# A two-layer encoder on one core: differential values as one 512-wide product, pinned products in the FFN units, decays by minimum, and x added by an accumulating transfer

## The chip, the core and the metric

The kernel runs on one core of one Trainium2 chip. The metric is device microseconds of one execution. The three runs of the kernel before gave 1241.12, 1241.12 and 1242.99 us, a median of 1241.12; the execution that was profiled took 1242.97 us, of which 1241.2 us are the span from its first to its last instruction. The engines are named as the profile names them: PE multiplies matrices (PEld is its weight load), DVE works on vectors, ACT evaluates functions and copies, POOL and SP issue transfers here (POOL also fills memory with constants).

## What is computed

The reference is an encoder trunk of two layers on 512 tokens of width 1024, in float32:

```python
h = rms_norm(x, attn_norm_g[l])
rq, rk, rv, rg, dq, dk, dv = split(h @ w_in[l])             # seven projections, each 512 wide
ret = retention_bidir(rq, rk / 8, rv, lg_f, lg_b)            # 8 heads of 64, two decays per head
ret = rms_norm(ret, ret_norm_g[l]) * silu(rg)
da  = diff_attention(norm(dq), norm(dk), dv, lam, slopes)    # 4 heads: (A1 - lam * A2) v
da  = rms_norm(da, diff_norm_g[l]) * (1 - lam_init)
x = x + concat(ret, da) @ w_out[l]
h = rms_norm(x, ffn_norm_g[l])
x = x + (silu(h @ w_gate[l]) * (h @ w_up[l])) @ w_down[l]    # 2816 hidden columns
```

In retention the score of query t and key s is multiplied by `exp(lg_f * (t - s))` where s is not after t, and by `exp(lg_b * (s - t))` where it is; both exponents are negative or zero.

## The kernel before

The stream x lies transposed, as eight tiles of 128 features by 512 tokens. Every float32 operand of a product is split into a rounded high part and a low part (a copy on ACT, a subtraction on DVE), and a product is three matmuls, high by high, high by low and low by high (`mm3`, lines 207 to 209). A chunk of weights, 128 by 1024, is loaded by SP, cast by ACT (L194) and subtracted by DVE (L200).

A layer runs like this.

- **First projections.** Key and query tiles 0 and 1 of the differential attention (`project_first`), four PSUM banks over four chunks, while the squares of x are summed for the norm. The norm's scale `rstd` comes after them.
- **Early part.** `qk_tile` evicts such a bank (L372: u is the bank times `rstd`), sums the squares of each head's 64 rows on PE (L139, L140, into an aux bank), and scales and splits the tile. Behind the four tiles stand the first half of the differential values (`project_dv(0)`: weights 256 columns wide are the moving operand, the tokens of h are the stationary one) and two of the four gate projections.
- **Heads.** Each of four differential heads goes through four blocks of 128 queries. A block has two score products (L406, two matmuls each) into the two `sc` banks; DVE evicts each with its bias and a running minimum (L410), ACT exponentiates; after the softmax the block is transposed on PE (L422), split, and multiplied with the values. Between blocks stand "fillers", one step of a projection each: query and key tiles 2 and 3, the second half of the values, gates 2 and 3, and the first retention projections. `project_k` and `project_q` end a step with the projection; the eviction (the first line of `qk_tile`) belongs to the next step.
- **Retention.** Four pairs of heads (`ret_pair`), each in four steps. A pair's decays are `exp` of an argument made from two constant arrays (`ndist`, `dpos`; lines 478 to 484, on DVE). Fillers are the last retention projections and the attention half of the output projection (`project_out(0)`), eight tiles whose product is added on DVE to a tile of x that SP has loaded (L643). Then comes the other half (`project_out(1)`), with the sums of the last pair's norm (L139, L140) among its products.
- **FFN.** Four hidden tiles are done plainly; eighteen others in units of seven products of 256 columns (`seven`, matmuls on L803): six hidden tiles, then a second group's first tile, four down units, five tiles, a last group's first tile, four down units, and the rest. A unit uses one `acc` bank (pa) and one `sc` bank (px). In the left half of pa three products add up: g1·b11, copied by ACT (L808), then s2·t2, copied again (L811), then s3·t3, which DVE subtracts (L815). In the right half of px stands s1·t1, copied by ACT (L813). A hidden tile's result is later split for the down units (`first_parts`, `second_parts`, the casts on L753).

What sets the order: the program is written as generators, and a scheduler with a simulated timeline places every instruction on its engine's queue. Each engine then takes its queue in order. The scheduler respects data and a few added dependencies, so a text that is changed in one place moves instructions in others. Units are numbered by `turns[0]` from 1 in each layer.

Of the kernel before, what the change touches and what calls it, by code (L numbers as in the profile page):

```python
# [13 lines left out]
P = 128  # L14
D = 1024
T = 512
DEPTH = 2
# [31 lines left out]
CST_DIST, CST_DPOS, CST_QPOS = 0, 896, 1280  # L49
# [5 lines left out]
def encoder_kernel(ctx: ExitStack, tc: tile.TileContext, xT, wfirst, wsingle, wvv, wout, wgu, wdn, wds, prm, lam, cst, outT):  # L55
# [75 lines left out]
    dpos = cst_sb[:, CST_DPOS : CST_DPOS + 384]  # L131
# [145 lines left out]
    def prepare_small():  # L277
# [4 lines left out]
        used = prm_sb[:, PRM_DEC : PRM_DEC + 32]  # L282
        lam_sb = big("lam")
# [30 lines left out]
        consts.update(gk=gk, lg=lg, lamn=lamn, gq=gq, gd=gd, wk=wk, rs=rs)  # L314

    def layer(l, n1, h, x_src, first_raw):
# [27 lines left out]
        lg, lamn, gq, gd, wk, rs = (consts[k] for k in ("lg", "lamn", "gq", "gd", "wk", "rs"))  # L344
# [24 lines left out]
        def qk_tile(ps, col, early, stack):  # L369

            u = big("u")
            nc.vector.tensor_tensor(u, ps, rstd, op=ALU.mult)  # L372
# [10 lines left out]
        def project_v(which, half, get=acc_bank):  # L383

            w = [[t.rearrange("p (k f) -> p k f", f=256) for t in chunk(wvv[l, which, half, i])] for i in range(2)]
            for i in range(4):
                ps = get()[:, :256]
# [53 lines left out]
        def ret_pair(pr):  # L441
            qT, kT, v = rqs[pr], rks[pr], rv
            lgc = lambda d, hh: lg[:, l * 16 + d * 8 + 2 * pr + hh : l * 16 + d * 8 + 2 * pr + hh + 1]
            lgp = lambda d: lg[:, 32 + l * 8 + d * 4 + pr : 32 + l * 8 + d * 4 + pr + 1]
# [90 lines left out]
        def project_dv(half, get=acc_bank):  # L535
            for i, ps in project_v(1, half, get):
                hi = tpool.tile([P, 256], F32R, tag="dv", name=nm("dvh"), bufs=16)
                lo = tpool.tile([P, 256], F32R, tag="dv", name=nm("dvl"), bufs=16)
# [3 lines left out]
                if i % 2:  # L542
                    yield
# [51 lines left out]
        for _ in project_dv(0, out_bank):  # L595
            pass
# [31 lines left out]
        for _ in fillers(gate[:2]):  # L628
            pass
# [433 lines left out]
```

## Time and profile before

| what | value |
|---|---|
| median of three runs | 1241.12 us |
| profiled execution | 1242.97 us |
| its span | 1241.2 us |
| PE busy | 1231.5 us, 7954 matmuls |
| DVE busy | 990.4 us |
| ACT busy | 739.7 us |
| POOL busy | 80.6 us |
| TensorE clock granted | 1.000 |
| read from memory, written | 152.29 MB, 4.19 MB |

Of layer 0, the first projections end near 30 us, the heads run from 64 to about 190 us, retention to about 260 us, the plain hidden tiles to about 340 us and the units to about 560 us. Layer 1 repeats this some 615 us later.

How to read it: a row of the timeline has the start in microseconds, the duration, engine, line, operation, tiles (output, then inputs), shapes and count, and in brackets the idle time before it and what ended it. A matmul's recorded duration is longer than the distance to the next start, as matmuls are pipelined; so the distance between starts is the time that one costs. A row of grouped instructions ends in busy time and mean nanoseconds of one, and behind the second bar the idle time ahead of them.

### The profile page before, as it was taken

How to read it: one execution, taken by the hardware profiler on the slowest of the kernel's cores; microseconds unless marked ns; L12 is line 12 of the kernel's file. 1: busy time of each engine (PE TensorE's matmuls, PEld its weight loads, DVE VectorE, ACT ScalarE, POOL GpSimd, SP SyncE). 2: the span in 40 equal slices, each digit the busy share in tenths (PEclk: the TensorE clock that was granted, in tenths of full speed). 3: DMA queues.
4: the chain of work that ended last, by engine and by line, in shares of the span. 5: the costliest groups of instructions: out<-in, count | busy, mean ns of one | idle time of the engine just before them, and what ended most of it. 6: DMA issues, size and time to landing. Idle time of an engine off the chain costs nothing. (4 is left out here: it accounts for less than half of the span.)

```text
span 1241.2 us, 20513 instructions
## 1 busy us (share of the span) xinstructions
PE 1231.5 (99%) x7954; PEld 1111.5 (90%) x7954; DVE 990.4 (80%) x1638; ACT 739.7 (60%) x1282; POOL 80.6 (6%) x94
## 2 busy tenths in 40 slices
PE   9999999999999999999999999999999999999998
PEld 7878988788899999999888889987788999999997
DVE  6899768868978888887648997699689788798763
ACT  6778747555456556555538786465554565566551
POOL 1000000010011111110000000000100111111100
PEclk9999999999999999999999999999999999999999
DMA  7222122363266796793532122141632767867822
GB/s 262 85 68 69 50 83 81 118 162 102 64 164 161 156 222 158 164 220 99 166 111 85 52 85 64 56 136 63 175 102 69 176 148 179 205 161 182 207 78 94
DMA packets 67554, 157.82 MB, mean 127 GB/s; under 512 B 6144, under 2 KB 16640, under 8 KB 67456
## 3 DMA queue, kind: packets, MB, share of 16 engines
q1 hardware_dynamic: 52880, 130.90, 34.1%
q0 software_dynamic: 14144, 25.17, 12.4%
q8 instruction: 62, 1.02, 0.3%
q10 hardware_dynamic: 432, 0.44, 0.1%
q14 instruction: 36, 0.29, 0.1%
HBM read 152.29 MB, written 4.19 MB: 126 GB/s over the span
## 5 line engine op out<-in xcount | busy, mean ns | idle before, releaser
L194 ACT CAST hi<-raw 128x1024 fp32r<-128x1024 f32 (+2 forms) x115 | 113.5, 992 | 112.2 <-PE sc L208 42.4
L200 DVE TENSOR_TENSOR lo<-raw,hi 128x1024 fp32r<-128x1024 f32 (+2 forms) x116 | 132.6, 1147 | 30.9 <-ACT hi L194 30.5
L209 PE MATMUL acc<-h,lo 128*128 128x512 f32 (+1 forms) x344 | 135.0, 393 | 0.0
L208 PE MATMUL acc<-h,hi 128*128 128x512 f32 (+1 forms) x344 | 135.0, 392 | 0.0
L207 PE MATMUL acc<-h,hi 128*128 128x512 f32 (+1 forms) x344 | 134.7, 394 | 0.0
L803 PE MATMUL acc<-hi,hi 128*128 128x256 f32 x432 | 122.5, 284 | 0.9 <-ACT g L811 0.9
L803 PE MATMUL acc<-hi,lo 128*128 128x256 f32 x432 | 122.2, 283 | 0.0
L803 PE MATMUL acc<-lo,hi 128*128 128x256 f32 x432 | 122.2, 283 | 0.0
L760 DVE TENSOR_TENSOR lo<-s,hi 128x1024 fp32r<-128x1024 f32 (+1 forms) x78 | 88.9, 1140 | 39.0 <-ACT hi L759 38.9
L760 DVE TENSOR_TENSOR lo<-raw,hi 128x1024 fp32r<-128x1024 f32 (+1 forms) x78 | 89.0, 1141 | 30.7 <-ACT hi L759 26.4
L759 ACT CAST hi<-s 128x1024 fp32r<-128x1024 f32 (+1 forms) x78 | 76.6, 983 | 48.8 <-PE acc L803 37.7
L759 ACT CAST hi<-raw 128x1024 fp32r<-128x1024 f32 (+1 forms) x78 | 76.6, 982 | 41.4 <-PE acc L803 20.7
L803 PEld LDWEIGHTS acc<-hi,hi 128*128 128x128 f32 x432 | 82.9, 192 | 1.4 <-ACT g L811 1.3
L803 PEld LDWEIGHTS acc<-lo,hi 128*128 128x128 f32 x432 | 82.9, 192 | 0.1
L803 PEld LDWEIGHTS acc<-hi,lo 128*128 128x128 f32 x432 | 82.9, 192 | 0.0
L209 PEld LDWEIGHTS acc<-h,lo 128*128 128x128 f32 x344 | 65.0, 189 | 13.3
L207 PEld LDWEIGHTS acc<-h,hi 128*128 128x128 f32 x344 | 64.8, 189 | 13.4 <-DVE u L372 0.6
L208 PEld LDWEIGHTS acc<-h,hi 128*128 128x128 f32 x344 | 65.0, 189 | 12.9
L781 POOL DMA_DIRECT2D s<-in_wgu x36 | 43.5, 1207 | 433.3 <-DMA s<-in_wgu 243.6
L803 PE MATMUL sc<-b,s 128*128 128x256 f32 x480 | 69.0, 283 | 0.0
L803 PEld LDWEIGHTS sc<-b,s 128*128 128x128 f32 x480 | 62.6, 192 | 0.0
L106 ACT ACTIVATE sc<-sc,mx 128x512 f32<-128x512 f32 x64 | 46.0, 720 | 18.1 <-DVE mx L410 17.8
(260 smaller groups left out, 3713.1 us busy)
## 6 DMA issues: line engine op xcount, KB each, us to landing
s<-in_wgu SPq DMA_DIRECT2D x54, 512.0 KB, 5.5
s<-in_wgu POOLq DMA_DIRECT2D x36, 512.0 KB, 7.8
raw<-in_wgu SPq DMA_DIRECT2D x34, 512.0 KB, 4.8
raw<-in_wsingle SPq DMA_DIRECT2D x32, 512.0 KB, 3.6
raw<-in_wgu SPq DMA_DIRECT2D x36, 256.0 KB, 3.8
s<-in_wds SPq DMA_DIRECT2D x24, 384.0 KB, 3.4
raw<-in_wvv SPq DMA_DIRECT2D x16, 512.0 KB, 3.7
raw<-in_wout SPq DMA_DIRECT2D x16, 512.0 KB, 3.6
```

What stands on the lines that cost most here:

```text
L106: i = nc.scalar.activation(out, src, f, **kw).ins
L194: c = nc.scalar.copy(hi[:, s], raw[:, s])
L200: nc.vector.tensor_tensor(lo[:, s], raw[:, s], f32(hi[:, s]), op=ALU.subtract)
L207: first = nc.tensor.matmul(out, L[0], R[0], start=start, stop=False)
L208: nc.tensor.matmul(out, L[0], R[1], start=False, stop=False)
L209: nc.tensor.matmul(out, L[1], R[0], start=False, stop=stop)
L759: last_cast[0] = nc.scalar.copy(hi, raw).ins.name
L760: last_split[0] = nc.vector.tensor_tensor(lo, raw, f32(hi), op=ALU.subtract).ins.name
L781: nc.gpsimd.dma_start(sums, blocks[:, 0::3], accum_op=ALU.add)
L803: nc.tensor.matmul(ps[:, t], L[x1], R[x2], start=start and k + i == 0, stop=k == n // P - 1 and i == 2, skip_group_check=True)
```

## The change

- **Differential values 512 wide.** `project_dv` makes all 512 columns at once: four banks (two `o`, two `acc`), one per block of 128 tokens, over four chunks; it is run right after the first projections, one chunk ahead of the four `qk_tile` and one behind each. All four gates become fillers.
- **Evictions.** The four first tiles are evicted together, ahead of their `qk_tile`. `qk_tile` gets the evicted tile. For key tile 2 the eviction stands behind its own projection, ahead of the yield.
- **Pinned products, deferred splits.** In units 3 and 8, s1·t1 may start only after s2·t2. The `first_parts` of units 1, 2 and 12 are issued after the next unit's first four products.
- **Decays by minimum.** With d = t − s signed, the exponent is min(lg_f·d, −lg_b·d): a scaled copy on ACT and one operation on DVE per head.
- **x accumulated.** In the first half of the output projection ACT copies the bank into a tile, and POOL issues a transfer that adds the tile of x from memory to it.

```diff
+        nlgb = used[:, :16]
+        for l in range(DEPTH):
+            nc.vector.tensor_scalar(nlgb[:, l * 8 : l * 8 + 8], lg[:, l * 16 + 8 : l * 16 + 16], -1.0, None, op0=ALU.mult)
...
-        def qk_tile(ps, col, early, stack):
-
-            u = big("u")
-            nc.vector.tensor_tensor(u, ps, rstd, op=ALU.mult)
+        def qk_tile(u, col, early, stack):
             ss = aux_bank()
...
-            behind = big("behind")
-            nc.vector.tensor_tensor(behind[:, :384], ndist[:, C : C + 384], dpos, op=ALU.add)
             for hh in range(2):
                 arg = big("arg")
-                nc.vector.tensor_scalar(arg[:, :384], behind[:, :384], lgc(1, hh), -1.0, op0=ALU.mult, op1=ALU.mult)
-                nc.vector.scalar_tensor_tensor(arg[:, :384], dpos, lgc(0, hh), arg[:, :384], op0=ALU.mult, op1=ALU.add)
+                nc.scalar.activation(arg[:, :384], signed, AF.Copy, scale=lgm(hh))
+                nc.vector.scalar_tensor_tensor(arg[:, :384], signed, lgc(0, hh), arg[:, :384], op0=ALU.mult, op1=ALU.min)
                 func(arg[:, :384], arg[:, :384], AF.Exp)
...
-        def project_dv(half, get=acc_bank):
-            for i, ps in project_v(1, half, get):
...
+        def project_dv():
+            banks = [b() for b in (out_bank, out_bank, acc_bank, acc_bank)]
+            for c in range(4):
+                w = [t.rearrange("p (k f) -> p k f", f=512) for t in chunk(wdv[l, c])]
+                for i in ((2, 3, 0, 1) if c == 3 else range(4)):
+                    ps = banks[i]
+                    for k in range(2):
+                        kt = 2 * c + k
+                        mm3(ps, cut(h[kt], slice(None), slice(i * P, (i + 1) * P)), cut(w, slice(None), k), kt == 0, kt == KT - 1)
+                yield
+            dv[:] = [[None] * 4 for _ in range(2)]
+            for i in (2, 3, 0, 1):
+                ps = banks[i]
+                for half in range(2):
...
         def project_k(m):
             ps = project("dk", m)
-            yield
-            k[m] = qk_tile(ps, kgc, False, stack_two)
+            if m not in (2,):
+                yield
+            u = big("u")
+            nc.vector.tensor_tensor(u, ps, rstd, op=ALU.mult)
+            if m in (2,):
+                yield
+            k[m] = qk_tile(u, kgc, False, stack_two)
...
-        for (name, m), ps in zip(FIRST, first):
+        us = []
+        for ps in first:
+            us.append(big("u"))
+            nc.vector.tensor_tensor(us[-1], ps, rstd, op=ALU.mult)
+        early_dv = project_dv()
+        next(early_dv)
+        for i, ((name, m), u) in enumerate(zip(FIRST, us)):
             if name == "dk":
-                k[m] = qk_tile(ps, kgc, True, stack_two)
+                k[m] = qk_tile(u, kgc, True, stack_two)
             else:
-                q[m] = qk_tile(ps, gq[:, l, m : m + 1], True, stack_one)
-        for _ in project_dv(0, out_bank):
-            pass
+                q[m] = qk_tile(u, gq[:, l, m : m + 1], True, stack_one)
+            next(early_dv, None)
...
-        for _ in fillers(gate[:2]):
-            pass
...
-                [project_k(2), project_q(2), project_k(3), project_q(3), project_dv(1)]
-                + gate[2:]
+                [project_k(2), project_q(2), project_k(3), project_q(3)]
+                + gate
...
+                products(m, (3,) if m < early else (0, 1, 2, 3))
                 if half == 0:
-                    x.append(load_x(x_src, m))
-                products(m, (3,) if m < early else (0, 1, 2, 3))
-                residual(m, x[m], ps[m], *then)
+                    x.append(big("x", tag="qk", bufs=NQK))
+                    nc.scalar.copy(x[m], ps[m])
+                    nc.gpsimd.dma_start(x[m], x_src[m], accum_op=ALU.add)
+                else:
+                    residual(m, x[m], ps[m], *then)
...
-            product(pa, H1, s2, "t2", False)
+            done = product(pa, H1, s2, "t2", False)
             nc.scalar.copy(g[:, H2], pa[:, H1])
-            product(px, H2, s1, "t1", True)
+            product(px, H2, s1, "t1", True, done if number in (3,8) else None)
...
-                    if not (j == 0 and wait):
+                    if not (j == 0 and wait) and turns[0] - 1 not in (1,2,12):
                         later.pop()()
...
             next(unit)
+            if later and i in (1,2,12):
+                later.pop()()
             if i + 1 < len(units):
                 next(units[i + 1])
...
-        [ndist, np.maximum(d, 0), qpos, np.eye(P), kpos], 1
+        [ndist, d, qpos, np.eye(P), kpos], 1
```

With the new argument `behind`, `product` adds a dependency on the named matmul to each of its own. The weights of the values are laid out as four chunks of two feature tiles by 512 columns.

**PE in unit 3 of layer 0.** The bank pa is acc_3777 before and acc_3671 in the change, px is sc_3778 and sc_3672. Before, all of s1·t1 stood ahead of s2·t2, and s3·t3 follows s2·t2 at once:

```order
L803 MATMUL sc_3778<-hi_3426,lo_3766 128x256
L803 MATMUL acc_3777<-hi_3160,hi_3761 128x256
L803 MATMUL acc_3777<-lo_3161,hi_3761 128x256
L803 MATMUL acc_3777<-hi_3160,lo_3762 128x256
L803 MATMUL acc_3777<-hi_3261,hi_3761 128x256
L803 MATMUL acc_3777<-lo_3262,hi_3761 128x256
L803 MATMUL acc_3777<-hi_3261,lo_3762 128x256
```

In the change, g1·b11 on acc_3671 ends in the first two of these rows, two matmuls of the unit before (acc_3541) follow, and then s2·t2 begins:

```order
L829 MATMUL acc_3671<-bl_3310,hi_3655 128x256
L829 MATMUL acc_3671<-bh_3309,lo_3656 128x256
L829 MATMUL acc_3541<-lo_3325,hi_3533 128x256
L829 MATMUL acc_3541<-hi_3324,lo_3534 128x256
L829 MATMUL acc_3671<-hi_3054,hi_3655 128x256
L829 MATMUL acc_3671<-lo_3055,hi_3655 128x256
```

Behind its twelve matmuls now stand the twelve of s1·t1 on sc_3672, and only then s3·t3.

**ACT in unit 2 of layer 0.** Before, a chunk's cast and the cast of the earlier tile's first part stand ahead of the copy out of px (the copy is the row with sc):

```order
L811 COPY g_3649<-acc_3647 128x256
L759 CAST hi_3761<-raw_3752 128x1024
L753 CAST b_3705<-u_3703 128x256
L813 ACTIVATE u_3650<-sc_3648 128x256
L759 CAST hi_3765<-s_3751 128x1024
```

and in the change:

```order
L840 COPY g_3543<-acc_3541 128x256
L842 ACTIVATE u_3544<-sc_3542 128x256
L785 CAST hi_3655<-raw_3646 128x1024
L779 CAST b_3638<-u_3597 128x256
L785 CAST hi_3659<-s_3645 128x1024
```

The copy moved ahead of both casts. In unit 12 it likewise moved ahead of the first part's cast.

**PE in the first head of layer 0.** Before, four pairs of score products follow each other, and then the projection of key tile 3 starts:

```order
L209 MATMUL acc_815<-h_172,lo_812 128x512
L406 MATMUL sc_740<-khi_397,q_426 128x512
L406 MATMUL sc_740<-klo_398,q_426 128x512
L406 MATMUL sc_747<-khi_403,q_427 128x512
L406 MATMUL sc_747<-klo_404,q_427 128x512
L406 MATMUL sc_843<-khi_397,q_426 128x512
L406 MATMUL sc_843<-klo_398,q_426 128x512
L406 MATMUL sc_850<-khi_403,q_427 128x512
L406 MATMUL sc_850<-klo_404,q_427 128x512
L207 MATMUL acc_899<-h_101,hi_895 128x512
```

and in the change, where the projection behind them is that of query tile 3:

```order
L406 MATMUL sc_807<-khi_439,q_496 128x512
L406 MATMUL sc_807<-klo_440,q_496 128x512
L406 MATMUL sc_814<-khi_445,q_497 128x512
L406 MATMUL sc_814<-klo_446,q_497 128x512
L422 MATMUL aux_665<-cst_sb,sc_648 128x128 x4
L406 MATMUL sc_889<-khi_439,q_496 128x512
L406 MATMUL sc_889<-klo_440,q_496 128x512
L406 MATMUL sc_896<-khi_445,q_497 128x512
L406 MATMUL sc_896<-klo_446,q_497 128x512
L422 MATMUL aux_726<-cst_sb,sc_709 128x128 x4
L207 MATMUL acc_963<-h_101,hi_959 128x512
```

The transposes of the first two query blocks moved in among the scores of the third and fourth; layer 1 has the same order.

More of the change, by code (lines that the diff above doesn't have):

```diff
@@ L130, in encoder_kernel @@
     ndist = cst_sb[:, CST_DIST : CST_DIST + 896]
-    dpos = cst_sb[:, CST_DPOS : CST_DPOS + 384]
+    signed = cst_sb[:, CST_SIGNED : CST_SIGNED + 384]
     qpos = cst_sb[:, CST_QPOS : CST_QPOS + 512]
@@ L381, in qk_tile, with project_v @@
             return stack(u, *(("qk", NQK) if early else ("mix", NMIX)))
-        def project_v(which, half, get=acc_bank):
-            w = [[t.rearrange("p (k f) -> p k f", f=256) for t in chunk(wvv[l, which, half, i])] for i in range(2)]
+        def project_v(half):
+            w = [[t.rearrange("p (k f) -> p k f", f=256) for t in chunk(wrv[l, half, i])] for i in range(2)]
             for i in range(4):
-                ps = get()[:, :256]
+                ps = acc_bank()[:, :256]
                 for kt in range(KT):
@@ L533, in layer @@
         rks, rqs, gates = [], [], []
[L535 to L543 removed]
+        def project_dv():
[12 more added lines that the diff above has]
+                for half in range(2):
+                    f = slice(half * 256, (half + 1) * 256)
+                    hi = tpool.tile([P, 256], F32R, tag="dv", name=nm("dvh"), bufs=16)
+                    lo = tpool.tile([P, 256], F32R, tag="dv", name=nm("dvl"), bufs=16)
+                    nc.scalar.activation(hi, ps[:, f], AF.Copy, scale=rstdc[:, i : i + 1])
+                    nc.vector.scalar_tensor_tensor(lo, ps[:, f], rstdc[:, i : i + 1], f32(hi), op0=ALU.mult, op1=ALU.subtract)
+                    dv[half][i] = hi, lo
         def project_rv(half):
[L546 removed]
+            for i, ps in project_v(half):
                 t = tpool.tile([P, 256], F32, tag="dv", name=nm("rv"), bufs=16)
@@ L795, in seven, with product @@
             s4 = cut(split_to(s4, [big("s4", F32R, "mix", NMIX)[:, :n] for _ in range(2)]), slice(None))
-            pa, px = acc_bank(), sc_bank()
-            def product(ps, t, w, r, start):
+            pa, px, number = acc_bank(), sc_bank(), turns[0]
+            def product(ps, t, w, r, start, behind=None):
                 for k in range(n // P):
@@ L802, in product @@
                     for i, (x1, x2) in enumerate(((0, 0), (0, 1), (1, 0))):
-                        nc.tensor.matmul(ps[:, t], L[x1], R[x2], start=start and k + i == 0, stop=k == n // P - 1 and i == 2, skip_group_check=True)
+                        mm = nc.tensor.matmul(ps[:, t], L[x1], R[x2], start=start and k + i == 0, stop=k == n // P - 1 and i == 2, skip_group_check=True)
+                        if behind:
+                            tc.add_manual_dep(mm.ins, behind, order, reason="product by product")
+                return mm.ins.name
             g, u = big("g"), big("u")
```

32 lines of the change are left out of this document (14 added, 18 removed).

## The prediction

> **What bounds the kernel now.** I read the page first: one core, and TensorE (PE) is busy for nearly the whole span.
>
> ```profile
> span 1241.2 us, 20513 instructions
> PE 1231.5 (99%) x7954; PEld 1111.5 (90%) x7954; DVE 990.4 (80%) x1638; ACT 739.7 (60%) x1282; POOL 80.6 (6%) x94
> ```
>
> So time falls in two ways only: fewer microseconds of matmul, or fewer places where PE waits. The span is a sum of matmul starts, and a start-to-start distance is read from stretches in which PE has one kind of work. The view of stretches gives, per row: length, then busy time and instructions of PE, weight loads, DVE, ACT, POOL, then granted clock.
>
> ```profile
> 280.00:320.00 40.00, 40.00 (x178) 33.10 (x177) 34.60 (x55) 23.13 (x34) 0.00 (x0) 1.00 0.33 105
> 1080.00:1120.00 40.00, 40.00 (x336) 40.00 (x335) 33.86 (x54) 25.34 (x45) 4.94 (x5) 1.00 0.68 164
> 34.00:63.70 29.70, 29.70 (x168) 25.96 (x167) 25.78 (x47) 23.60 (x40) 0.00 (x0) 1.00 0.27 87
> 63.70:92.00 28.30, 27.34 (x142) 21.95 (x140) 26.76 (x58) 20.28 (x43) 0.00 (x0) 1.00 0.23 75
> 198.90:257.50 58.60, 58.60 (x324) 45.43 (x322) 51.70 (x83) 32.05 (x51) 4.62 (x6) 1.00 0.44 130
> ```
>
> The first is the 512-wide gate and up products: 40.00/178 = 224.7 ns per matmul. The second is the 256-wide combined units: 40.00/336 = 119.0 ns. Two 256-wide matmuls cost 238.0 ns, so a 512-wide one that does the same work saves 13.3 ns. The clock is 1.00 in both. The third and fourth rows are the wait for the first scores and the first two heads, the last is retention: there PE is busy 58.60 of 58.60 us.
>
> Next the view of waits, for PE alone: who was waited for, total, times, longest.
>
> ```profile
> PE acc L803 <- ACT g L811: 1.4, 4, 0.5
> PE acc L803 <- ACT g L808: 0.6, 2, 0.3
> PE acc L207 <- DVE u L372: 0.5, 1, 0.5
> PE aux L140 <- DVE lo L226: 0.4, 1, 0.4
> PE sc L803 <- ACT u L813: 0.3, 2, 0.2
> ```
>
> These are small, and PE loses more than they show, since a busy matmul record outlasts the next start. So I take the true loss from start times in the timeline.
>
> **The change, part by part.**
>
> *Differential values 512 wide.* Each layer drops 192 matmuls of 256 columns and gets 96 of 512. Over two layers that is 384 × 119.0 = 45.7 us out and 192 × 224.7 = 43.1 us in: **−2.5 us**, on PE, which has no idle time to hide it in. The ends are small here, 2.3 to 2.8 for a nanosecond either way per matmul. The evictions stay eight scaled copies and eight subtractions of 256 columns per layer.
>
> The Trainium skill (TensorE: Matmul & The Clock Gate, section "Wait — 56ns, not 53.3ns?") has N columns take N ÷ 2.4 GHz plus about 2.5 ns, 109.2 and 215.8 ns, so by it the widening would return only 0.5 us. The two stretches disagree with that; the measured spacing decides, and the rule gets no chance of its own.
>
> *Combined units: products pinned, splits deferred.* Four places of layer 0, pairs of matmuls on either side of a gap:
>
> ```profile
> 360.25 0.28 PE L803 MATMUL acc<-bl,hi 128*128 128x256 f32 x1
> 360.52 0.38 PE L803 MATMUL sc<-bh,hi 128*128 128x256 f32 x1
> ...
> 368.90 0.28 PE L803 MATMUL acc<-hi,lo 128*128 128x256 f32 x1
> 369.64 0.39 PE L803 MATMUL acc<-hi,hi 128*128 128x256 f32 x1 [0.46 <-ACT g L811]
> ...
> 419.06 0.40 PE L803 MATMUL sc<-h,hi 128*128 128x256 f32 x2
> 419.68 0.38 PE L803 MATMUL acc<-h,hi 128*128 128x256 f32 x1 [0.23 <-ACT g L811]
> ...
> 461.17 0.28 PE L803 MATMUL acc<-hi,lo 128*128 128x256 f32 x1
> 461.62 0.39 PE L803 MATMUL sc<-bh,hi 128*128 128x256 f32 x1 [0.17 <-ACT u L813]
> ```
>
> They belong to units 2, 3, 8 and 12. Distance less normal spacing (two spacings for the x2 row) is 0.15, 0.62, 0.38 and 0.33 us; the matmul behind each gap is itself 0.1 us longer, so I count 0.25, 0.72, 0.48 and 0.43. The counts in the waits (four for L811, two for L813) show the same places in layer 1. Units 3 and 8 wait for ACT to copy a partial sum out of the bank into which the next product is to be added. In unit 8 the change puts the nine matmuls of another bank there, 9 × 0.119 = 1.1 us, which covers 0.48: gone. In unit 3 twelve matmuls go between the second and third products, but the order of the changed program then has the first and the second product on the same bank with only two foreign matmuls between. So the wait moves one product forward: 0.72 − 2 × 0.12 = 0.48 remains, and 0.24 is won. In units 2 and 12 ACT's copy of the other bank stands behind a cast of the earlier activation; in the new order it stands ahead of it, and 0.25 and 0.43 go. ACT's deferred casts land where PE has a unit's products to do, and are needed only in the down units. Per layer 0.25 + 0.24 + 0.48 + 0.43 = 1.4: **−2.8 us**, with 0 (every wait moves on) and −3.8 (none comes back) as the ends.
>
> *Early part of a layer.* From the first value product to the first score:
>
> ```profile
> 30.74 0.28 PE L207 MATMUL o<-hi,h 128*128 128x256 f32 x1
> ...
> 63.67 0.39 PE L406 MATMUL sc<-khi,q 128*128 128x512 f32 x1
> ```
>
> 32.9 us; now 96 value matmuls, 23 of a projection and eight sums stand there, 119 × 0.2247 + 8 × 0.225 = 28.5 us. Scores come 4.4 us sooner, and two gates fill the heads in place of the second half of the values, at nearly equal PE and DVE work. What PE loses in the heads, two gaps of layer 0 and one of layer 1:
>
> ```profile
> 67.97 0.39 PE L406 MATMUL sc<-klo,q 128*128 128x512 f32 x1
> 68.75 0.50 PE L406 MATMUL sc<-khi,q 128*128 128x512 f32 x1 [0.39 <-DVE mx L410]
> ...
> 91.05 0.39 PE L406 MATMUL sc<-klo,q 128*128 128x512 f32 x1
> 91.92 0.39 PE L207 MATMUL acc<-hi,h 128*128 128x256 f32 x1 [0.48 <-DVE u L372]
> ...
> 703.64 0.63 PE L422 MATMUL aux<-cst_sb,sc 128*128 128x128 f32 x4
> 704.75 0.50 PE L406 MATMUL sc<-khi,q 128*128 128x512 f32 x1 [0.48 <-DVE mx L410]
> ```
>
> 0.55 + 0.64 + 0.76 (four transposes normally take 0.35) = 1.95 us. The first comes from four pairs of scores in a row on two banks; in the new order four transposes stand amid them, which cover 0.35 of about 0.55. The other two come where DVE is full (26.76 of 28.30 us). There the four raw tiles are now evicted at once and key tile 2 right behind its projection, before the scores' work rather than among it. But the fill after query tile 3 must wait for that tile's eviction, some 0.5 us by its place in DVE's order. I take **−1.2 us**, with −1.9 and a loss of 3 (below) as the ends.
>
> *End of layer 1's retention.* The last pair's norm:
>
> ```profile
> 873.33 0.40 PE L209 MATMUL sc<-hi,lo 128*128 128x512 f32 x1
> 873.86 0.50 PE L139 MATMUL aux<-hi,bones_r 128*128 128x512 f32 x1
> 874.73 0.51 PE L140 MATMUL aux<-lo,bones_r 128*128 128x512 f32 x1 [0.38 <-DVE lo L226]
> 875.08 0.39 PE L207 MATMUL acc<-hi,hi 128*128 128x512 f32 x1
> ```
>
> 0.30 + 0.64 + 0.12 = 1.1 us. Only six products stood between the last values and the sums; now twelve do in both layers, 12 × 0.2247 = 2.7 us, against a square, a cast and a subtraction:
>
> ```profile
> L146 ACT ACTIVATE sq<-o 128x512 f32<-128x512 f32 x16 | 9.5, 596 | 18.8 <-PE o L510 11.3 <-PE o L209 7.4
> ...
> L225 ACT CAST hi<-sq 128x512 fp32r<-128x512 f32 x48 | 29.4, 617 | 13.3 <-DVE sq L526 12.3 <-DVE sq L437 0.5
> ...
> L226 DVE TENSOR_TENSOR lo<-sq,hi 128x512 fp32r<-128x512 f32 x48 | 32.9, 686 | 19.9 <-ACT hi L225 19.3
> ```
>
> 0.596 + 0.617 + 0.686 = 1.9 us, which fits: **−1.1 us**, ends 0 and −1.1.
>
> *Decays by minimum, x accumulated.*
>
> ```profile
> L643 DVE TENSOR_TENSOR x<-x,acc 128x512 f32<-128x512 f32 x33 | 22.3, 680 | 2.9 <-PE acc L209 2.7
> L425 ACT CAST ah<-aux 128x512 fp32r<-128x512 f32 x32 | 18.5, 580 | 19.7 <-PE aux L422 19.5
> s<-in_wgu POOLq DMA_DIRECT2D x36, 512.0 KB, 7.8
> ```
>
> Per layer DVE loses eight additions (8 × 0.68 = 5.4 us) and the decay steps; ACT gets eight copies out of PSUM (0.58 each by the nearest row, 4.6 us) and eight scalings. ACT was busy 32.05 of 58.60 us there, DVE 51.70, and PE never stood still, so this costs and gains nothing: **0**. The cover is the two acc banks and PE's other work; with it gone each copy is 0.6 us on PE, 8 per layer, 9.6 us in all. SP loses the x loads; nothing stood behind them that was late. On POOL the eight transfers stand ahead of the third and fourth memsets of the last pair, which have some ten microseconds. An accumulating transfer of this kind into x is not in the trace: below, a plain load; above, the 7.8 us of twice the bytes from POOL's queue. The last x is first read some 26 us of PE work after its copy, so either end is hidden.
>
> Sum: −2.5 − 2.8 − 1.2 − 1.1 = **−7.6 us**, made against the profiled span of 1241.2 (that execution took 1242.97; the three runs have a median of 1241.12, so profile and runs differ by what lies around the span). Taken off the median: **1233.5 us**.
>
> **Rivals.** *The heads get worse* (0.18): scores come 4.4 us sooner, and DVE was idle only 3.9 us in the 29.7 us ahead of them. If it can't use these for the extra value splits, PE waits for scores: say 1.5 us more per layer than now, 1241.1 − 6.4 + 3.0 = 1237.7. Against it: the first tiles' DVE work up to the first score, added up in its new order, is some 22 us from the norm's end, three less than PE's. *The waits only move* (0.10): ACT is in order, and a pinned product or an earlier copy leaves another one late, as unit 3 half shows. Then only the widening counts: 1241.1 − 2.5 = 1238.6. *Late x, slower than before* (0.05): a residual of the second half waits for an accumulating transfer, holds its bank, and PE stops ahead of the FFN. It decides once a transfer takes over 26 us from its copy, against 7.8 for twice the bytes; at 35 us it costs 9 us per layer, 1241.1 − 7.6 + 18 = 1251.5. *No wait returns* (0.05): −2.5 − 3.8 − 1.9 − 1.1 = −9.3, 1231.8.
>
> The Trainium skill (SBUF — State Buffer, section "SBUF: two separate sides", its box on DVE blocking DMA) has a transfer from POOL's queue starve while DVE runs certain copies; that would be a cause of the late x. No run here shows one, and retention's DVE work is mostly two-input operations.
>
> **How the numbers follow.** The forecast has 0.62; its own range, from half the gain in heads and units to nearly all, is 1231.5 to 1236. Time: **1233.5**. For 8 in 10 the range takes in nearly all of the forecast, most of the worse heads and of the best case: **1230.0 to 1238.0**. Within 0.2% (2.5 us, about what can be told from no change) means above 1238.6. Faster: 0.62 + 0.05 + 0.15 of the worse heads + 0.04 of the moved waits = 0.86. Same: 0.03 + 0.06 = 0.09. Slower: 0.05.
>
> **What would show it.** The value products as 192 matmuls of 128x512, spaced as the others. In the units, gaps at units 2, 8 and 12 gone, and one of about 0.5 us in unit 3 between its first and second products. No gap before the last pair's norm in layer 1. In the heads fewer microseconds of PE waiting on L410's successor; if PE waits before the first scores, the forecast's third term is wrong. If PE waits on x's residual, the last is.

## The result, and the profile after

The changed kernel takes 1231.95 us (median of 6 runs, 1231.68 to 1232.39), the kernel before 1241.16 on the same chip. The ratio is 0.9923, with a 95% interval of 0.9911 to 0.9936: 9.2 us faster, where 7.6 were forecast.

The head of the page after, and its waits of PE (columns as in the prediction):

```profile
span 1229.8 us, 20149 instructions
PE 1223.7 (99%) x7762; PEld 1099.6 (89%) x7762; DVE 970.8 (79%) x1600; ACT 755.7 (61%) x1314; POOL 94.1 (8%) x110
...
PE acc L829 <- ACT g L837: 1.0, 4, 0.3
```

PE has 192 matmuls fewer and is as full as before. Of the five waits quoted from the profile before one kind is left, with another line: four waits of L829 for L837, ACT's copy behind a unit's first product (L808 before, two waits). The same view of the kernel before has a longer row, which the prediction does not quote, PE's wait for DVE to read the scores out of their bank:

```profile
PE sc L406 <- DVE mx L410: 1.5, 4, 0.5
```

After, it has no such row: the four waits are gone.

To see where the time went, I cut each layer at three matmuls that both kernels have: the norm's first sum (L139), the first matmul of the combined units, and the last one. From the timeline of PE, before and then after (start in us, busy, engine, line, operation):

```profile
30.27 0.40 PE L139 MATMUL aux<-hi,ones_r 128*128 128x512 f32 x1
339.75 0.28 PE L803 MATMUL acc<-bh,hi 128*128 128x256 f32 x1
589.48 0.28 PE L803 MATMUL acc<-hi,lo 128*128 128x256 f32 x1
643.62 0.40 PE L139 MATMUL aux<-hi,ones_r 128*128 128x512 f32 x1
955.38 0.28 PE L803 MATMUL acc<-bh,hi 128*128 128x256 f32 x1
1205.11 0.28 PE L803 MATMUL acc<-hi,lo 128*128 128x256 f32 x1
```

```profile
28.14 0.40 PE L139 MATMUL aux<-hi,ones_r 128*128 128x512 f32 x1
335.54 0.28 PE L829 MATMUL acc<-bh,hi 128*128 128x256 f32 x1
583.89 0.28 PE L829 MATMUL acc<-hi,lo 128*128 128x256 f32 x1
638.03 0.40 PE L139 MATMUL aux<-hi,ones_r 128*128 128x512 f32 x1
945.40 0.28 PE L829 MATMUL acc<-bh,hi 128*128 128x256 f32 x1
1193.76 0.28 PE L829 MATMUL acc<-hi,lo 128*128 128x256 f32 x1
```

| stretch | before | after | difference |
|---|---|---|---|
| start to norm, layer 0 | 30.27 | 28.14 | −2.13 |
| norm to units, layer 0 | 309.48 | 307.40 | −2.08 |
| units, layer 0 | 249.73 | 248.35 | −1.38 |
| units to norm, layer 1 | 54.14 | 54.14 | 0 |
| norm to units, layer 1 | 311.76 | 307.37 | −4.39 |
| units, layer 1 | 249.73 | 248.36 | −1.37 |

The first row is no effect of the change. The profiled execution of before took 1242.97 us, 1.8 above its median, and lost that at the very start (shown in the last section). So these 1.8 us lie inside the span, not around it as the prediction has it; the forecast does not depend on that. The start needs no change for it: in a profile of the kernel before with nothing but the units changed (below) the norm starts at 28.66 us. Without this row the others add up to −9.22 us, which is the difference of the medians. Of that, −2.75 lie in the units and −6.47 ahead of them, where 2.8 and 4.8 were forecast (2.5 + 1.2 + 1.1). So what I had too small is ahead of the units, by 1.7 us.

### The profile page after: what moved, and what is told of

The parts are those of the page before. It is cut to its first block, busy times and chain, and to the rows that moved or that the text cites. A ratio compares the mean times of both kernels' runs of the same rounds, so it can differ in the third digit from the quotient of the medians.

```text
span 1229.8 us, 20149 instructions
## 1 busy us (share of the span) xinstructions
PE 1223.7 (99%) x7762; PEld 1099.6 (89%) x7762; DVE 970.8 (79%) x1600; ACT 755.7 (61%) x1314; POOL 94.1 (8%) x110
## 5 line engine op out<-in xcount | busy, mean ns | idle before, releaser
L200 DVE TENSOR_TENSOR lo<-raw,hi 128x1024 fp32r<-128x1024 f32 (+2 forms) x116 | 132.4, 1147 | 33.4 <-ACT hi L194 32.9
L829 PE MATMUL acc<-hi,hi 128*128 128x256 f32 x432 | 122.5, 284 | 0.5 <-ACT g L837 0.5
L829 PE MATMUL acc<-hi,lo 128*128 128x256 f32 x432 | 122.2, 283 | 0.0
L829 PE MATMUL acc<-lo,hi 128*128 128x256 f32 x432 | 122.2, 283 | 0.0
L786 DVE TENSOR_TENSOR lo<-s,hi 128x1024 fp32r<-128x1024 f32 (+1 forms) x78 | 88.9, 1140 | 38.5 <-ACT hi L785 38.4
L829 PEld LDWEIGHTS acc<-hi,hi 128*128 128x128 f32 x432 | 82.9, 192 | 0.9 <-ACT g L837 0.9
L829 PEld LDWEIGHTS acc<-lo,hi 128*128 128x128 f32 x432 | 82.9, 192 | 0.1
L829 PEld LDWEIGHTS acc<-hi,lo 128*128 128x128 f32 x432 | 82.9, 192 | 0.0
L829 PE MATMUL sc<-b,s 128*128 128x256 f32 x480 | 69.3, 283 | 0.0
L829 PEld LDWEIGHTS sc<-b,s 128*128 128x128 f32 x480 | 62.8, 192 | 0.0
L106 ACT ACTIVATE sc<-sc,mx 128x512 f32<-128x512 f32 x64 | 46.0, 720 | 25.7 <-DVE mx L410 25.6
```

The costliest lines, as they stand in the source:

```text
L106: i = nc.scalar.activation(out, src, f, **kw).ins
L200: nc.vector.tensor_tensor(lo[:, s], raw[:, s], f32(hi[:, s]), op=ALU.subtract)
L786: last_split[0] = nc.vector.tensor_tensor(lo, raw, f32(hi), op=ALU.subtract).ins.name
L829: mm = nc.tensor.matmul(ps[:, t], L[x1], R[x2], start=start and k + i == 0, stop=k == n // P - 1 and i == 2, skip_group_check=True)
```

## The experiments

Each was timed against the kernel before on the same chip. Times are medians, and the changed kernel's 1231.95 is what they are compared with unless another is named. The kernel before lay between 1241.16 and 1241.45 us on these chips, so 0.3 us can be a matter of the chip. For the stretch from norm to units I name the layers' lengths, since that sorts a difference to its place.

### Units: pins and deferred splits taken off, and put on alone

```diff
-            product(px, H2, s1, "t1", True, done if number in (3,8) else None)
+            product(px, H2, s1, "t1", True, done if number in () else None)
...
-                    if not (j == 0 and wait) and turns[0] - 1 not in (1,2,12):
+                    if not (j == 0 and wait) and turns[0] - 1 not in ():
...
-            if later and i in (1,2,12):
+            if later and i in ():
```

> The changed kernel with neither pins nor deferred splits in the combined units. My theory (four gaps per layer, 0.25 + 0.72 + 0.48 + 0.43 us in the profile before, of which 0.48 stayed in unit 3): 1.4 us per layer come back, 1231.95 + 2.8 = 1234.7 us, with waits of PE on ACT's copies at units 2, 3, 8 and 12 again. Rival (the early part moved the units' surroundings too, so that some of these gaps would be gone without the pins): below 1.4 us in all, and fewer than four gaps per layer.

Measured: 1234.76 us, 2.8 slower. The waits of PE are those of the kernel before, row for row in count and length:

```profile
PE acc L829 <- ACT g L840: 1.4, 4, 0.5
PE acc L829 <- ACT g L837: 0.6, 2, 0.3
PE sc L829 <- ACT u L842: 0.3, 2, 0.2
```

The other way round, the same three edits put into the kernel before and nothing else:

> The kernel before with the change's pins (units 3 and 8) and deferred splits (units 1, 2 and 12) alone. My theory (the units' waits are local: they don't depend on what the layer's first part does): 2.8 us faster than the kernel before, 1238.5 us, with one wait of 0.49 us left in unit 3 of each layer. Rival (part of the 2.8 us that came back in the changed kernel without them belongs to the other edits' timing): less than 1.8 us.

Measured: 1238.50 us against 1241.33, 2.8 faster (ratio 0.9981, 0.9972 to 0.9990). Its units take 248.35 us per layer as in the changed kernel, and its stretches from norm to units 309.49 and 311.72 us as in the kernel before. So this term is local, and it adds to the others. The pin of unit 8 and the three deferred splits were not taken off one by one.

### The pin of unit 3 alone

```diff
-            product(px, H2, s1, "t1", True, done if number in (3,8) else None)
+            product(px, H2, s1, "t1", True, done if number in (8,) else None)
```

> The changed kernel without the pin in unit 3 (unit 8 keeps its pin, the deferrals stay). My theory (the pin only moves unit 3's wait one product forward, and wins two foreign matmuls, 0.24 us): the gap goes back to between the second and the third product and grows from 0.49 to 0.72 us, 0.5 us in two layers: 1232.4 us. Rival A (the pin is what also keeps ACT's later copies in time): a further gap in units 4 or 5, 1 us or more. Rival B (the order without the pin is just as good now): 0, with the one gap of 0.49 us in another place.

Measured: 1231.86 us, no difference. I had 0.5 us. Unit 3 does not wait at all without its pin, since its s1·t1 stands between its first and its second product again; but the first unit of the down products, unit 8, now waits between its first and its second product:

```profile
410.26 0.28 PE L829 MATMUL acc<-b,lo 128*128 128x256 f32 x1
411.06 0.50 PE L829 MATMUL acc<-h,hi 128*128 128x256 f32 x2 [0.52 <-ACT g L837]
```

0.80 − 0.12 = 0.68 us, and 0.10 on the next matmul. The 0.23 us that the changed kernel loses in unit 10 went with it, so the two sums are 0.72 and 0.78 us per layer. The pin in unit 3 chooses the place of the wait, not its size: the rival "the waits only move" holds for this pin.

### Two pairs of pins more

In the changed kernel two waits per layer are left between the first product (b11) and the second (t2) of a unit, at units 3 and 18. In unit 3 only two matmuls, of the unit before, stand between the first product and the second, whose first matmul must wait for ACT's copy of that bank:

```profile
361.56 0.28 PE L829 MATMUL acc<-hi,lo 128*128 128x256 f32 x1
362.07 0.38 PE L829 MATMUL acc<-hi,hi 128*128 128x256 f32 x1 [0.23 <-ACT g L837]
```

The unit before still has a whole product (t4) to do. The edit holds it back so that it stands between:

```diff
-            product(pa, H1, g1, "b11", True)
+            b11_last[0] = product(pa, H1, g1, "b11", True)
...
-            done = product(pa, H1, s2, "t2", False)
+            done = product(pa, H1, s2, "t2", False, t4_last[0] if number in (3, 18) else None)
...
-            product(pa, H1, u2, "t4", False)
+            t4_last[0] = product(pa, H1, u2, "t4", False, b11_last[0] if number in (2, 17) else None)
```

> The changed kernel with two pairs of pins more: unit 2's last product on the acc bank is held behind unit 3's first product, and unit 3's second product behind that one; the same for units 17 and 18. My theory: the waits of units 3 (0.39 + 0.10 us) and 18 (0.44 + 0.10 us) of the changed kernel each need about 0.75 us of foreign matmuls between the first and the second product, and 12 x 0.120 = 1.4 us are put there: 1.03 us per layer, 2.06 us in all: 1229.9 us. Rival (waits only move, as the run with the pin in unit 3 taken off showed, where the gap of unit 3 went and one of 0.78 us came in unit 8): some other unit waits instead, 1231.0 us or more.

Measured: 1230.09 us, 1.9 less than the changed kernel and 11.2 less than the kernel before (ratio 0.9907, 0.9892 to 0.9922). No wait of the units is left in the view of waits; its two rows, of which this is one, belong to the start of the program:

```profile
PE acc L207 <- ACT h L218: 0.2, 1, 0.2
```

So a wait of this kind can be removed where foreign work is at hand; that one pin moved it and two pins removed it is a matter of having twelve matmuls (1.4 us) and not two between the products. A third pin, in unit 10, was tried on top:

```diff
-            product(px, H2, s1, "t1", True, done if number in (3,8) else None)
+            product(px, H2, s1, "t1", True, done if number in (3,8,10) else None)
```

> The changed kernel with the two pairs of pins (units 2 to 3 and 17 to 18) and a third pin like that of units 3 and 8 in unit 10, whose first product on the sc bank starts 0.13 + 0.10 us late in the changed kernel since that bank is still being read. My theory: with nine products of another bank ahead of it 0.23 us per layer are won besides the 2 us of the two pairs: 1229.6 us. Rival (the wait moves to another unit): 1230.1 us or more.

Measured: 1229.99 us, the same as without it. The 0.23 us that unit 10 lost on its sc bank is lost on its acc bank instead, 0.37 − 0.12 = 0.25 us ahead of the second product:

```profile
425.90 0.28 PE L829 MATMUL acc<-b,lo 128*128 128x256 f32 x1
426.27 0.50 PE L829 MATMUL acc<-h,hi 128*128 128x256 f32 x2
```

The rival was right there: the two matmuls that were pinned away had been the cover of the acc bank's copy.

### Differential values in 256-wide matmuls again

```diff
-                        mm3(ps, cut(h[kt], slice(None), slice(i * P, (i + 1) * P)), cut(w, slice(None), k), kt == 0, kt == KT - 1)
+                        for f in (slice(0, 256), slice(256, 512)):
+                            L, R = cut(h[kt], slice(None), slice(i * P, (i + 1) * P)), cut(w, slice(None), k, f)
+                            for j, (x1, x2) in enumerate(((0, 0), (0, 1), (1, 0))):
+                                nc.tensor.matmul(ps[:, f], L[x1], R[x2], start=kt + j + f.start == 0, stop=kt == KT - 1 and j == 2, skip_group_check=True)
```

> The changed kernel, but each 512-wide product of the differential values is issued as two 256-wide ones into the two halves of the same bank: 192 matmuls of 128x256 per layer again, everything else as in the changed kernel. My theory (the stretches of the profile before: 119.0 ns per 256-wide matmul, 224.7 ns per 512-wide): two layers lose 2.5 us, so 1231.95 + 2.5 = 1234.5 us, spread over the value products, with no new gap in the heads. Rival A (the gain in the layers' first part, 5.4 us by the two profiles against the 3.7 I had counted, comes from the wide products altogether, since half as many weight loads and issues are needed): 4 us or more, 1236 us or more. Rival B (the widening gave nothing by itself and the other edits closed the gaps): below 0.8 us.

Measured: 1238.01 us, 6.06 slower, in the range of rival A. Whether it was also rival A's cause was left to a second run of the same kernel, for its profile:

> The same kernel as in the first run of this label's name, for an undisturbed profile: its runs lay 6.06 us above the changed kernel, where I had expected 2.5. Theory A (a 256-wide product that changes the half of its bank after every three matmuls takes longer than 119 ns): spacing of the narrow value products near 131 ns, since (6.06 + 192 x 0.227) / 384 = 0.129, and no gap in the heads. Theory B (the spacing is 120 ns and costs 2.5 us, and the other 3.5 us are waits of PE in the heads, because the first scores come later again, as before the change): spacing 120 ns, and gaps of PE that sum to some 1.8 us more per layer than in the changed kernel, behind the first scores.

Measured: 1237.80 us. The narrow value products are 120.0 ns apart (187 distances per layer, 22.45 us in all), and PE waits in places where the changed kernel doesn't:

```profile
PE o L208 <- DVE al L426: 1.4, 2, 0.7
...
PE acc L207 <- DVE dvl L555: 0.6, 2, 0.4
136.53 0.36 PE L207 MATMUL o<-ah,dvh 128*128 128x256 f32 x1
137.60 0.38 PE L208 MATMUL o<-al,dvh 128*128 128x256 f32 x1 [0.71 <-DVE al L426]
```

So the spacing is theory B's, 2.5 us by width, and rival A's cause is out. The stretch from norm to units is 310.59 and 310.03 us, 3.2 and 2.7 above the changed kernel; 1.25 of each are the width, and 0.95 the wait at 136.53 (its like comes in layer 1). The wait of a projection for the values' evictions (the row with L555) adds little, since the changed kernel loses some 0.9 us at the same place, the first four blocks of scores (shown in the section on the prediction). Instead 0.7 us per layer are lost in retention. From its first value product (`o<-sm,rv`) to the matmul behind the last it takes 36.75 us, with 12 matmuls of 512 columns fewer in between than the 38.76 us of the changed kernel; with these, at 0.227 us each, it would be 39.5. So theory B had only part of the rest right, and in one point it was wrong: the first score does not come later here but earlier, 25.7 us behind the norm's first sum against 30.1, since the order was planned anew. Undoing one part of a planned program undoes part of the plan too; the 6.06 us are no price of the width.

### The heads: three edits of the changed kernel undone one by one

The first tiles evicted one by one, each ahead of its own norm work:

```diff
-        us = []
-        for ps in first:
-            us.append(big("u"))
-            nc.vector.tensor_tensor(us[-1], ps, rstd, op=ALU.mult)
...
+            u = big("u")
+            nc.vector.tensor_tensor(u, ps, rstd, op=ALU.mult)
             if name == "dk":
```

> The changed kernel, but the four raw tiles of the first projections are not evicted at once: each is evicted when its own norm work begins, as before the change. My theory (eviction ahead of the scores' work is one of the two things that closed the heads' gaps, 1.4 us per layer): one of the gaps returns, 0.6 us per layer, 1233.2 us. Rival A (the early scores alone closed them, so the order of the evictions does nothing): 1231.95, within 0.3. Rival B (the wide value products need the two acc banks that raw tiles hold, so late evictions stop PE ahead of the scores): a wait of the value products on DVE, over 1 us per layer, 1234 us or more.

Measured: 1233.70 us, 1.75 slower. The loss is in layer 0 alone (309.22 us from norm to units; layer 1 has 307.17). As in rival B, PE stops ahead of the scores, but not at the value products: it stops at a norm's sums, whose aux bank DVE still reads (L379), and at a projection, whose acc bank the values' last evictions still read:

```profile
53.84 0.50 PE L139 MATMUL aux<-hi,bones_r 128*128 128x512 f32 x1 [0.85 <-DVE sq L379]
55.59 0.47 PE L207 MATMUL acc<-h,hi 128*128 128x512 f32 x1 [1.02 <-DVE dvl L552]
```

The kernel before had no such stop, and none of its waits on L410 came back. So this edit does not close the gaps in the heads; it keeps a new stop away that the other edits would bring in layer 0.

Key tile 2 evicted at its turn, not behind its projection:

```diff
-            if m not in (2,):
+            if m not in ():
...
-            if m in (2,):
+            if m in ():
```

> The changed kernel, but key tile 2 is evicted as the other tiles of the heads are, at its turn in the fill, not behind its projection. My theory (this eviction is a part of what closed the heads' gaps, as the early eviction of the four first tiles is, which returned 1.75 us when it was taken off): one gap of some 0.5 us per layer returns, 1233.0 us. Rival (the early scores and the first tiles did it alone): 1231.95, within 0.3 us.

Measured: 1234.60 us, 2.65 slower. The stretch from norm to units is 308.65 us in both layers, 1.25 and 1.28 more, and one wait per layer explains it:

```profile
67.74 0.50 PE L406 MATMUL sc<-khi,q 128*128 128x512 f32 x1 [1.34 <-DVE mx L410]
```

PE reaches the next scores before DVE has read the last ones out of their bank. The pairs of scores follow each other without transposes between them, as before the change. So the place of one eviction is worth 2.65 us; by which steps of DVE's order it delays that reading was not followed further.

The first two gates projected ahead of the heads, as before the change:

```diff
+        for _ in fillers(gate[:2]):
+            pass
         weave(
...
-                + gate
+                + gate[2:]
```

> The changed kernel, but the first two gates are projected ahead of the heads, as before the change, so the heads are filled by two gates fewer and the scores come two projections (48 matmuls x 0.227 = 10.9 us) later by the written order. My theory: the heads need these fillers where the second half of the values was before; without them PE waits for the softmax at the heads' end, 1 us or more per layer: 1234 us or more. Rival (there is filler enough from the retention projections, and DVE has more time ahead of the first scores): 1231.95, within 0.5, or faster.

Measured: 1242.69 us, 10.7 slower, more than the whole gain of the change. The late scores were not the cost (the first comes 30.3 us behind the norm, against 30.1), but the lack of fill at the heads' end was:

```profile
PE sc L406 <- DVE mx L410: 4.9, 2, 2.4
PE aux L422 <- DVE rz L414: 1.6, 2, 1.0
```

These are 6.5 us. The profiled execution took 1244.23 us, 12.5 more than that of the changed kernel; the rest is told in the last section: the clock fell.

### x loaded and added, decays as before

```diff
-                    x.append(big("x", tag="qk", bufs=NQK))
-                    nc.scalar.copy(x[m], ps[m])
-                    nc.gpsimd.dma_start(x[m], x_src[m], accum_op=ALU.add)
-                else:
-                    residual(m, x[m], ps[m], *then)
+                    x.append(load_x(x_src, m))
+                residual(m, x[m], ps[m], *then)
```

> The changed kernel, but x is loaded and the first output half is added to it on DVE, as before the change. My theory: the eight additions per layer (0.68 us each) and the eight copies on ACT are both off PE's path, so 0; the 1.1 us at the end of layer 1's retention stays won if twelve products still stand between the last values and the sums: 1231.95 us, at most 0.3 off. Rival (DVE, busy 51.70 of 58.60 us in retention before, is what the last pair's norm waited for, so the additions matter): the gap before the last pair's sums comes back, 1 us in layer 1 or in both: 1233.0 to 1234.1 us.

Measured: 1232.05 us, no difference; norm to units 307.42 and 307.47 us.

```diff
+            behind = big("behind")
+            nc.vector.tensor_tensor(behind[:, :384], ndist[:, C : C + 384], signed, op=ALU.add)
...
-                nc.scalar.activation(arg[:, :384], signed, AF.Copy, scale=lgm(hh))
-                nc.vector.scalar_tensor_tensor(arg[:, :384], signed, lgc(0, hh), arg[:, :384], op0=ALU.mult, op1=ALU.min)
+                nc.vector.tensor_scalar(arg[:, :384], behind[:, :384], lgc(1, hh), -1.0, op0=ALU.mult, op1=ALU.mult)
+                nc.vector.scalar_tensor_tensor(arg[:, :384], signed, lgc(0, hh), arg[:, :384], op0=ALU.mult, op1=ALU.add)
...
-        [ndist, d, qpos, np.eye(P), kpos], 1
+        [ndist, np.maximum(d, 0), qpos, np.eye(P), kpos], 1
```

> The changed kernel with the decays of the kernel before: one addition and one scaling more on DVE per head pair, no scaling on ACT, and a sum in place of the minimum. My theory: off PE's path, 0; the order of the retention products moves a little with it, and each run of values that is cut differently costs 0.1 to 0.2 us, so 1231.95 within 0.6. Rival (DVE sets the pace of retention, and its 0.5 us per pair are seen by PE): 1 us or more per layer, 1234 us or more, with waits of PE on masked scores.

Measured: 1231.70 us, no difference beyond the runs' spread. Yet its profile has the wait at the end of retention again, now in both layers:

```profile
864.01 0.50 PE L139 MATMUL aux<-hi,bones_r 128*128 128x512 f32 x1
864.89 0.50 PE L140 MATMUL aux<-lo,bones_r 128*128 128x512 f32 x1 [0.38 <-DVE lo L226]
```

Six products stand between the last values and the sums here, as in layer 1 before the change, and the stretch behind the last values is 1.1 us longer again. But the last values start 223.7 us behind the norm's first sum instead of 224.8, and from norm to units both layers take 307.3 us. So this run has two effects of 1.1 us that cancel. The second lies among retention's value products, which are issued in groups with other matmuls between: 64 per layer, in six groups here and in eight in the changed kernel. From the first of them to the matmul behind the last this kernel takes 34.45 us, with 12 matmuls of 512 columns and four of 256 fewer in between; with these it would be 37.7, 1.1 less than 38.76. That the groups are the reason is not shown.

## Why the prediction was right, and where it was off

The time (1231.95, forecast 1233.5, range 1230.0 to 1238.0) and the sign were right. The time is also next to the 1231.8 of the rival "no wait returns", but that is chance: one wait did return in unit 3, the heads kept some 0.9 us of gaps per layer and gave more than that rival allowed. Step by step:

- **The widening, −2.5.** Right. The second run of the narrow kernel has 120.0 ns between its narrow products; 384 of these less 192 of 227 ns (the distance of the 512-wide ones in the changed kernel's timeline) is 2.5 us. My 119.0 and 224.7 ns were 1% low, since a view of stretches counts the matmuls that straddle both ends; the difference of the two was not touched. The Trainium skill's rule (TensorE: Matmul & The Clock Gate, section "Wait — 56ns, not 53.3ns?") would have given 0.5 us; these distances, 13 to 14 ns over N ÷ 2.4 GHz and not 2.5, do not agree with it here.
- **Units, −2.8.** Right as a sum, and by places: −1.38 and −1.37 us per layer against 1.4. Units 2, 8 and 12 have no wait left. Unit 3's wait moved to between its first and second product, and the next matmul starts 0.51 us later instead of 0.12: 0.39 + 0.10 on the matmul behind it is 0.49, against the 0.48 forecast. But that the pin of unit 3 wins 0.24 was not borne out: without it the wait leaves unit 3 and comes to unit 8 at about the same price.
- **Early part and heads, −1.2.** The mechanism was right, the term too small by half. Ahead of the units the layers got 2.08 and 4.39 us shorter. Less the widening's 1.25 each, and 1.05 for layer 1's tail, 0.83 and 2.09 remain, together 2.9. Not all of that lies in the heads. From retention's first value product to the matmul behind the last, layer 1 has the same numbers of matmuls of each width before and after, and yet:

```profile
832.44 1.08 PE L510 MATMUL o<-sm,rv 128*64 128x256 f32 x8
872.07 0.50 PE L207 MATMUL sc<-hi,hi 128*128 128x512 f32 x1
...
824.38 1.51 PE L509 MATMUL o<-sm,rv 128*64 128x256 f32 x10
863.14 0.50 PE L207 MATMUL sc<-hi,hi 128*128 128x512 f32 x1
```

  This takes 39.63 us before and 38.76 after, 0.9 less; layer 0 takes 42.27 before, with 17 matmuls of 512 columns more in between, so 38.4 without these, and 38.76 after, 0.3 more. So retention, which the prediction put at 0 but for the tail, gave 0.5 us net. The cause stays open; the value products stand in eight groups in layer 0 and in nine in layer 1 before, in eight after. Some 2.4 us remain for the early part and the heads.

  The step that failed is the count of the gaps: I took three, 1.95 us, and set some 0.75 against them for a new wait of the fill behind query tile 3. Two of the three are waits on L410, and the view of waits has four. The other two, in layer 1, I left out (timeline of before):

```profile
681.35 0.39 PE L406 MATMUL sc<-klo,q 128*128 128x512 f32 x1
682.08 0.50 PE L406 MATMUL sc<-khi,q 128*128 128x512 f32 x1 [0.34 <-DVE mx L410]
682.42 0.40 PE L406 MATMUL sc<-klo,q 128*128 128x512 f32 x1
683.09 0.50 PE L406 MATMUL sc<-khi,q 128*128 128x512 f32 x1 [0.27 <-DVE mx L410]
683.43 0.40 PE L406 MATMUL sc<-klo,q 128*128 128x512 f32 x1
```

  They are 0.50 + 0.11 + 0.44 + 0.11 = 1.16 us over the normal 0.227. Around all these places further delays of 0.1 to 0.3 us, about 1.2 us in all, were not counted either, so some 4.3 us stood there before. The new wait did not come, but the changed kernel keeps a loss at the first four blocks of scores, the same in both layers:

```profile
72.07 0.60 PE L422 MATMUL aux<-cst_sb,sc 128*128 128x128 f32 x4
...
73.84 0.66 PE L422 MATMUL aux<-cst_sb,sc 128*128 128x128 f32 x4
...
74.84 0.40 PE L208 MATMUL acc<-h,hi 128*128 128x512 f32 x1
```

  Eight transposes and five products of 512 columns stand there in 2.77 us; by the prediction's 0.35 us for four transposes and 0.227 us for a product they would take 1.84, so 0.9 is lost per layer. So 4.3 us became 1.9, which is the 2.4 us less; I had 1.2.

  The eviction of key tile 2 decides this: undone, one gap on L410 per layer returns, and 2.65 us. The common eviction of the first tiles is another matter, since its 1.75 us are a stop ahead of the scores that the kernel before did not have. The scores came 3.3 us sooner behind the first value product (29.6 us instead of 32.9), not 4.4; the rival that they come too soon for DVE did not happen.
- **End of layer 1's retention, −1.1.** The gap is gone and the stretch behind the last values is 1.05 us shorter. The run with the old decays bears out the reason: with six products there, the gap is back in both layers, and so are the 1.1 us behind the last values. That the layer is no longer in that run is due to another 1.1 us won earlier in retention, which the prediction did not have.
- **Decays and x, 0.** Right for the time by both runs, 0.1 and −0.25 us, though for the decays the 0 is two effects that cancel. The late x did not happen: the transfers take 4.1 us to land (median of eight), the last starts at 249.52, and DVE reads the first x at 264.5, in the stage where they are due:

```profile
x<-in_xT POOLq DMA_DIRECT2D x8, 256.0 KB, 4.1
249.52 0.86 POOL L695 DMA_DIRECT2D x<-in_xT  x1 [7.65 <-ACT x L694]
```

## What to carry to other kernels

On an engine that never idles, time is lost in pieces of 0.2 to 0.7 us, and start-to-start distances find them where the view of waits shows half; count all of them, in every layer, before pricing an edit, and check the count against the number of waits that the view gives: it had four waits on L410 here, and two of them were priced. A wait between two products into one bank goes away when enough foreign work (here 1.4 us of it against a need of 0.75) is put between them, and only moves when less is. When a part is undone in a program whose order is planned as a whole, compare the profiles stretch by stretch before the difference is called the price of that part.

## What was not expected of the hardware

**A PE that pauses is slow afterwards.** In the run with the gates ahead, PE stood still for 2.43 us in layer 0, did four matmuls, and stood still for 1.02 us more. In the view of stretches (columns as in the prediction, the clock is the first number behind POOL) the granted clock then falls to half, for nearly seven microseconds:

```profile
132.00:136.00 4.00, 1.35 (x5) 0.60 (x4) 2.61 (x9) 3.35 (x9) 0.00 (x0) 1.00 0.00 0
136.00:138.00 2.00, 1.21 (x5) 1.08 (x6) 1.96 (x6) 0.39 (x1) 0.00 (x0) 0.50 0.00 0
140.00:142.00 2.00, 2.00 (x11) 2.00 (x10) 1.89 (x5) 1.19 (x3) 0.00 (x0) 0.50 0.00 0
```

There 256-wide matmuls start 213 ns apart instead of 120. In layer 1 the clock is at half before the second pause comes, so there the first was enough:

```profile
750.01 0.50 PE L406 MATMUL sc<-khi,q 128*128 128x512 f32 x1 [2.43 <-DVE mx L410]
...
750.40:750.60 0.20, 0.20 (x2) 0.00 (x0) 0.20 (x3) 0.20 (x1) 0.00 (x0) 0.50 0.00 0
```

PE works for about six microseconds per layer at half speed, which is 3 us lost; twice that and 6.5 us of waits make the 12.5 us of the profiled execution. The other runs of this kernel fit: of the eleven, the two with a mean granted clock of 0.997 took 1241.64 and 1241.95 us, the five with 0.994 took 1242.96 to 1244.23. The Trainium skill (TensorE: Matmul & The Clock Gate, section "Part 1: The HAM clock gate") has the clock halved after an idle window of about 3.4 us. This run agrees with the half clock, but a single pause of 2.43 us was enough here.

**The same thing at the start is why the profiled execution of before was 1.8 us above its median.** Its first products, and then the changed kernel's:

```profile
8.52 0.63 PE L208 MATMUL acc<-h,hi 128*128 128x512 f32 x1
8.95 0.63 PE L209 MATMUL acc<-h,lo 128*128 128x512 f32 x1
```

```profile
7.29 0.39 PE L208 MATMUL acc<-h,hi 128*128 128x512 f32 x1
7.51 0.39 PE L209 MATMUL acc<-h,lo 128*128 128x512 f32 x1
```

They are 0.43 us apart in the one until 10.2 us, 0.22 in the other from about 5 us on, both with a first matmul at 1.47 us. The same section of the Trainium skill has the full clock come after some 3.4 us of work, at a point that varies from run to run; the changed kernel's 3.5 us agree with that, the 8.7 us of before are far longer. Of the fourteen profiles of this case twelve reach full speed by about 5 us; the other late one is that of the narrow kernel's first run, with 0.43 us between products until 11 us. The column of the granted clock says 1.00 for both, so here only the distances tell. Single runs of before lie near 1241.2 or near 1243.0, which fits this, but the starts of the unprofiled runs are not on record. A profile whose start was cold must be compared with another from a matmul behind the start, as the table above does.
